# Two edits to a two-layer encoder trunk: four modulation dot products per plain tile of the first feed-forward part, and weight copies in program order on ACT in the last pair of the others

## The chip, the cores and the metric

The kernel runs on one core of one Trainium2 chip. It is one launch, and its time is what the device takes for it, in microseconds (us). A core has a matrix engine (PE, with its weight loads shown apart as PEld), a vector engine (DVE), a scalar engine (ACT), GpSimd (POOL) and a sync engine (SP), whose queue issues nearly all the transfers here. Each engine takes its own instructions in a fixed order, and semaphores hold an instruction until what it needs is there. Matmuls read their operands from SBUF and sum into PSUM.

## The reference

The input x is 512 rows of 1024 numbers. It passes through two layers; each is feed-forward, mixer, feed-forward. The mixer of layer 0 is a bidirectional Mamba-2 SSD, that of layer 1 is latent attention (MLA). The kernel counts these six sublayers as s = 0 (feed-forward), 1 (SSD), 2 and 3 (feed-forward), 4 (MLA), 5 (feed-forward). What matters here is the feed-forward and the modulation:

```python
D_MODEL, SEQ, DEPTH, D_FF = 1024, 512, 2, 2816

def modulate(x, g, shift, scale):
    return rms_norm(x, g) * (1.0 + scale[:, None, :]) + shift[:, None, :]

def swiglu(h, w_gate, w_up, w_down):
    return (jax.nn.silu(h @ w_gate) * (h @ w_up)) @ w_down

cond = jax.nn.silu(c)
for i in range(DEPTH):
    mod = (cond @ w_mod[i] + b_mod[i]).reshape(-1, 3, 3, D_MODEL)
    h = modulate(x, norm_g[i, 0], mod[:, 0, 0], mod[:, 0, 1])
    x = x + 0.5 * mod[:, 0, 2][:, None, :] * swiglu(h, ffn_w_gate[i, 0], ffn_w_up[i, 0], ffn_w_down[i, 0])
    h = modulate(x, norm_g[i, 1], mod[:, 1, 0], mod[:, 1, 1])
    x = x + mod[:, 1, 2][:, None, :] * mixer(h)
    h = modulate(x, norm_g[i, 2], mod[:, 2, 0], mod[:, 2, 1])
    x = x + 0.5 * mod[:, 2, 2][:, None, :] * swiglu(h, ffn_w_gate[i, 1], ffn_w_up[i, 1], ffn_w_down[i, 1])
```

Everything is float32. So `w_mod` is 2 x 1024 x 9216 numbers, 75 MB, and each of its 18,432 columns is used once, against one vector.

## The kernel before, in words

**Arithmetic.** A float32 product is made of three matmuls (`mm3`, L366 to L368): each operand is a high part plus a low part, and high x high, high x low and low x high are summed. The weights arrive as float32 (`raw`), ACT copies the high part (L169, a CAST to the matmul's type), and DVE subtracts it from `raw` to get the low part (L170).

**Weight units.** All weights are one long list of units of at most 128x1024 numbers (class `Units`). A unit is loaded by a transfer that SP issues (L113, at most three places `raw`, tag `raw`), then split by ACT and DVE into one of four places of a ring (`w`, RING = 4), and the matmuls read it there. So a split has to wait until the matmuls have let go of the unit four places earlier.

**A feed-forward sublayer** (`ffn`) goes through its 22 tiles of 128 hidden columns in four parts of 6, 6, 6 and 4 tiles (FF_PIECES; `pi` counts the parts). In a part, first the gate and up projections of its tiles, then their share of the down projection: eight output tiles into `dacc` for the first three parts, added to the residual X by DVE (L461), and `last()` (`lacc`) for the fourth, which also starts the next sublayer's norm. There are two ways for gate and up. A *plain* tile has two units (gate, up) and 24 matmuls of 512 columns for each, into `pgu`; then `gated` (silu on ACT, multiply L831 and low part L833 on DVE, high part L832 on ACT). A *pair* (`pair`, L784 to L815) does two tiles together in seven block products (`blk`) in place of eight, whose weights are sums of units: `cut_pair` makes them with ACT copies at L147 and DVE subtractions at L148. Its results `gs` go through silu (L802), a multiply (L803), the high part by ACT (L804) and the low part by DVE (L805) into `u`. The first sublayer (s = 0) uses plain tiles alone; s = 2, 3 and 5 use pairs from their fourth tile on. So "last pair" (`pi` = 3, `i` = 2) exists in s = 2, 3 and 5 alone. The four units of the down projection in `last()` go to places of their own (`wl`, tag `last`).

**Modulation.** The 144 dot products of `cond` with `w_mod` (8 blocks of 128 columns for each of 18 vectors) are DVE work: each is a transfer of 512 KB into `mraw` (L262, issued by SP, two places) and one multiply-and-sum over 128x1024 (L268), with a short read of the accumulator behind it. They are handed out in *ticks*: TICKS[s] = (dot products per plain tile, per pair, per output tile of the down projection). They stand in program order among themselves (`keep_in_program_order`), so that the transfers and the dot products keep their sequence. Each sublayer needs its own 24 before its norm and its gate; `finish_side` sees to that.

**Order of the work.** A scheduler orders each engine's instructions from the program, except where they are kept in program order, and in the first sublayer's start, which is written out by hand.

Of the kernel before, what the change touches and what calls it, by code (L numbers as in the profile page):

```python
# [22 lines left out]
FF_PIECES = (6, 6, 6, 4)  # L23
FF_MAX = max(FF_PIECES)
START = 3
TICKS = {0: (3, 1, 1), 2: (0, 0, 1), 3: (0, 0, 2), 5: (0, 0, 0)}
RIGHT = {0: (), 2: (), 3: (), 5: ()}
LATE = {4: 3, 2: 4}

# [47 lines left out]
class Units:  # L77
# [1 line left out]

    RAW_AHEAD, SPLIT_AHEAD = 3, 2  # L80

    def __init__(self, nc, raw_pool, w_pool):
        self.nc, self.raw_pool, self.w_pool = nc, raw_pool, w_pool
        self.todo, self.raw, self.split = [], {}, {}
        self.at = self.n_raw = self.n_split = 0
        self.held, self.in_ring = set(), {}
        self.places, self.over = {"raw": [], "raw4": []}, set()

    def add(self, src, n, kind="w"):
        self.todo.append((src, n, kind))  # L90
# [26 lines left out]
    def cut_pair(self, i, j, group, raw, t):  # L117
        nc = self.nc
        add, sub = nc.vector.tensor_add, nc.vector.tensor_sub
        minus = lambda out, x, y: nc.gpsimd.tensor_tensor(out, x, y, op=ALU.subtract)  # L120
        new = lambda: self.sum_pool.tile([P, 1024], F32, tag="sum", name="wsum", bufs=3)
        if raw is not None:
            group[j] = raw, i
        r = lambda j: group[j][0]
        if j < 2:
            x = raw
        elif j == 2:
            self.load(i + 2)
            group[3] = self.raw[i + 1], i + 1
            group["s1"], x = new(), new()  # L130
            group["s2"] = x
            add(group["s1"], r(2), r(3))
            (minus if "2" in POOL else sub)(x, group["s1"], r(0))
        elif j == 3:
            x = group["s1"]
        elif j == 4:
            x = new()
            (minus if "3" in POOL else sub)(x, r(0), r(2))
            self.over.update((group[0][1], group[2][1]))
        elif j == 5:  # L140
            x = new()
            (minus if "4" in POOL else sub)(x, r(1), group["s2"])
            self.over.add(group[1][1])
        else:
            x = r(3)
            self.over.add(group[3][1])
        nc.scalar.copy(out=t[:, 0], in_=x)  # L147
        (minus if "abcdefg"[j] in POOL else sub)(t[:, 1], x, t[:, 0].bitcast(F32))  # L148

    def cut(self, upto, early=False):  # L150
        while self.n_split < min(upto, len(self.todo)):
            i = self.n_split
            if self.todo[i][2] != "last":
                n = len(self.in_ring)
                if n - RING in self.held:
                    assert early, "a unit is wanted whose place is taken"
                    return
                self.in_ring[i] = n
            self.load(i + 1)
            _, n, kind = self.todo[i]  # L160
            raw = self.raw.pop(i)
            if kind != "last":
                t = self.w_pool.tile([P, 2, 1024], F32R, tag="w", name="w")
            else:
                t = self.last_pool.tile([P, 2, n], F32R, tag="last", name="wl")
            if isinstance(kind, tuple):
                self.cut_pair(i, *kind, raw, t)
            else:
                self.nc.scalar.copy(out=t[:, 0, :n], in_=raw[:, :n])  # L169
                self.nc.vector.tensor_sub(t[:, 1, :n], raw[:, :n], t[:, 0, :n].bitcast(F32))  # L170
                self.over.add(i)
            self.split[i] = t
            self.n_split += 1

    def next(self, ahead=True, hold=False):
        i = self.at
        self.at += 1
        self.load(i + 1)
        self.cut(i + 1)
        if hold:  # L180
            self.held.add(self.in_ring[i])
        if ahead:
            self.ahead()
        return self.split.pop(i)
# [19 lines left out]
class Trunk:  # L204
    def __init__(self, ctx, tc, d, subs):
        self.ctx, self.tc, self.nc, self.d = ctx, tc, tc.nc, d
        self.subs = subs
        pool = lambda name, **kw: ctx.enter_context(tc.tile_pool(name=name, **kw))
        self.const = pool("const", bufs=1)
        self.keep = pool("keep", bufs=1)  # L210
        self.raw_pool = pool("rawp", bufs=RAWS)
        self.w_pool = pool("wp", bufs=RING)
        self.units = Units(self.nc, self.raw_pool, self.w_pool)
        self.ps = pool("ps", bufs=3, space=PSUM)
        self.ps_c = pool("psc", bufs=3, space=PSUM)
        self.ps_s = pool("pss", bufs=2, space=PSUM)
        self.n_acc, self.wide = 0, False
# [424 lines left out]
    def ffn(self, s, nxt):  # L642
        nc, tc = self.nc, self.tc
        with ExitStack() as c:
# [28 lines left out]
            for pi, n in enumerate(FF_PIECES):  # L673
                for i in range(n):
                    if self.by_blocks(s, pi, i - i % 2):
                        if i % 2 == 0:
                            if self.factors == 0:
                                next(right)
                            self.pair(U[i:i + 2], wk, right)
                            self.ticks(TICKS[s][1])  # L680
                        continue
                    if first and pi == 0 and i < START:
                        self.gated(U[i], acc[2 * i], acc[2 * i + 1], full, wk)
                        self.ticks(TICKS[s][0])
                        continue
                    both = (i, i + 1) if pi == 0 and i == 0 else () if pi == 0 and i == 1 else (i,)
                    ws = [(self.units.next(), self.units.next()) for _ in both]
                    for ts in (halves if len(both) == 2 else (full,)):
                        nt = ts.stop - ts.start
                        for b, w in zip(both, ws):  # L690
                            pg, pu = (self.acc_tile("pgu") for _ in range(2))
                            self.norm_step(2 * b)
                            self.project(pg[:, :nt], w[0], ts)
                            if len(both) == 1:
                                self.ticks(TICKS[s][0] // 2)
                            self.norm_step(2 * b + 1)
                            self.project(pu[:, :nt], w[1], ts)
                            self.gated(U[b], pg, pu, ts, wk)
                    self.ticks(TICKS[s][0] - TICKS[s][0] // 2)
                    for _ in range(RIGHT[s].count((pi, i))):  # L700
                        next(right)
                while s not in self.gated_by:
                    self.tick()
                self.later = True
                if pi < len(FF_PIECES) - 1:

                    for ms in [(0, 1)] + [(m,) for m in range(2, KT)]:
                        part = []
                        for m in ms:
                            w = self.units.next()[:, :, :n * P].rearrange("p s (k c) -> p s k c", k=n)  # L710
                            part.append((w, self.acc_tile("dacc")))
                        for ks in (range(n - 1), (n - 1,)):
                            for w, ps in part:
                                for k in ks:
                                    self.mm3(ps, w, (k, slice(None)), U[k][0], U[k][1], k == 0, k == n - 1)
                        for m, (_, ps) in zip(ms, part):
                            self.residual(s, m, ps, full)
                            self.ticks(TICKS[s][2])
                else:
                    self.finish_side({0: 2, 2: 3, 3: 5, 5: 5}[s])  # L720
                    if nxt == 4:
                        v = self.rope.rearrange("p (n m) (c f) -> p n m c f", m=2, c=4)
                        self.tables = {"q": (v[:, 0, 0], v[:, 0, 1]), "k": (v[:, 1, 0], v[:, 1, 1])}
                        self.mla_tables()
                    self.last(s, nxt, n, lambda k: U[k])

    def right_tiles(self):
# [869 lines left out]
```

## Time and profile before

| | us |
|---|---|
| three timed runs: median (lowest to highest) | 2240.96 (2239.34 to 2241.18) |
| the profiled execution | 2238.92 |
| its span, first to last instruction | 2237.2 |
| PE busy in the span | 2192.6 (98%) |
| DVE busy | 1824.0 (82%) |
| ACT busy | 1109.3 (50%) |
| POOL busy | 239.7 (11%) |

The profiled execution is 1.7 us longer than its span, and 2.0 us below the median of the timed runs. Its mean granted TensorE clock was 0.991. The trace names a piece of work by its engine, its line and its tiles, as "PE dacc L368": a matmul of line 368 that writes `dacc`. SPq is SP's queue, where transfers are issued. "[4.20 <-ACT u L804]" behind an instruction says that its engine sat idle for 4.20 us and that ACT's write of `u` at line 804 ended it. The first sublayer's matmuls of `pgu` and `dacc` run from 65.6 us to 371.5 us of the span, in the parts `pgu` to 98.2, `dacc` to 132.1, `pgu` to 197.4, `dacc` to 230.0, `pgu` to 295.3, `dacc` to 328.0, `pgu` to 371.5.

### The profile page before, as it was taken

Reading aid. Unit: us, or ns where it says so; the run is one execution under the profiler, and the core shown is the slowest. Engines: PE = TensorE matmul, PEld = TensorE weight load, DVE = VectorE, ACT = ScalarE, POOL = GpSimd, SP = SyncE. Lnnn points to the kernel's source line nnn. Section 1 sums busy time; section 2 is a strip of 40 time slices with the busy share of each in tenths; the row PEclk is TensorE's granted clock in tenths of the full one; section 3 lists DMA queues with packets and bytes.
Section 4 is the critical chain, followed back from the end, with each engine's and each line's share of the span. In section 5 each row is a group of like instructions: output and inputs, shape, how many; then the busy total and the mean of one; then the engine's idle time right before and its main releaser. Section 6 shows DMA issues by size and latency. Waiting matters only on the chain.

```text
span 2237.2 us, 34479 instructions
## 1 busy us (share of the span) xinstructions
PE 2192.6 (98%) x13414; PEld 1932.0 (86%) x13414; DVE 1824.0 (82%) x2914; ACT 1109.3 (50%) x1890; POOL 239.7 (11%) x195
## 2 busy tenths in 40 slices
PE   8999999999999998999999999999999999999999
PEld 5888888878888877989999988899978888999989
DVE  7777667889888688889989879797779988877966
ACT  3322223687667675534435534353467875433433
POOL 0000000000000000010100001011046750011110
PEclk9999999999999999999999999999999999999999
DMA  8787776244434423253444144332220112333232
GB/s 297 224 276 249 234 248 222 85 128 142 132 122 134 141 95 120 90 168 114 169 161 160 58 141 137 109 100 90 78 68 14 39 39 76 97 102 104 93 105 76
DMA packets 87348, 292.93 MB, mean 131 GB/s; under 512 B 10192, under 2 KB 12880, under 8 KB 87184
## 3 DMA queue, kind: packets, MB, share of 16 engines
q1 hardware_dynamic: 86320, 288.79, 39.7%
q8 instruction: 105, 1.72, 0.3%
q10 hardware_dynamic: 864, 1.93, 0.2%
q14 instruction: 59, 0.48, 0.1%
HBM read 288.32 MB, written 2.36 MB: 130 GB/s over the span
## 4 chain that ended last, share of the span: by engine, by line
PE 83%; DVE 10%; DMA 3%; ACT 2%; issue 1%; POOL 1%; SPq 0%; ACTq 0%; DVEq 0%; POOLq 0%
PE blk L786 7%; PE blk L785 7%; PE blk L784 7%; PE dacc L368 5%; PE dacc L366 5%; PE dacc L367 5%; PE pgu L366 5%; PE pgu L367 5%; PE pgu L368 5%; PE inp L366 4%; PE inp L367 4%; PE inp L368 4%; DMA mraw<-in_wmod 2%; PE py L1075 2%; PE lacc L366 2%; PE oacc L366 2%
## 5 line engine op out<-in xcount | busy, mean ns | idle before, releaser
L169 ACT CAST w<-raw 128x1024 fp32r<-128x1024 f32 (+3 forms) x257 | 241.0, 945 | 343.9 <-PE dacc L368 110.4
L170 DVE TENSOR_TENSOR w<-raw,w 128x1024 fp32r<-128x1024 f32 (+3 forms) x257 | 280.0, 1095 | 49.9 <-ACT w L169 48.9
L786 PE MATMUL blk<-rf,w 128*128 128x256 f32 x864 | 245.7, 284 | 3.0 <-DVE w L148 3.0
L784 PE MATMUL blk<-rf,w 128*128 128x256 f32 x864 | 245.3, 284 | 0.8 <-ACT w L147 0.8
L785 PE MATMUL blk<-rf,w 128*128 128x256 f32 x864 | 245.2, 284 | 0.0
L268 DVE CUSTOM_DVE_ANT_0 mraw<-mraw,cond,small 128x1024 f32<-128x1024 f32 x144 | 182.4, 1280 | 54.1 <-DMA mraw<-in_wmod 53.8
L368 PE MATMUL dacc<-u,w 128*128 128x512 f32 x576 | 224.2, 389 | 0.6 <-DVE w L170 0.6
L367 PE MATMUL dacc<-u,w 128*128 128x512 f32 x576 | 224.3, 389 | 0.1
L366 PE MATMUL dacc<-u,w 128*128 128x512 f32 x576 | 224.2, 389 | 0.0
L366 PE MATMUL pgu<-Hhi,w 128*128 128x512 f32 (+1 forms) x592 | 208.4, 359 | 3.0 <-ACT Hhi L360 3.0
L368 PE MATMUL pgu<-Hhi,w 128*128 128x512 f32 (+1 forms) x592 | 210.2, 358 | 0.0
L367 PE MATMUL pgu<-Hlo,w 128*128 128x512 f32 (+1 forms) x592 | 209.8, 359 | 0.0
L786 PE MATMUL blk<-Hhi,w 128*128 128x256 f32 x648 | 183.4, 283 | 0.0
L785 PE MATMUL blk<-Hlo,w 128*128 128x256 f32 x648 | 183.4, 283 | 0.0
L784 PE MATMUL blk<-Hhi,w 128*128 128x256 f32 x648 | 183.3, 283 | 0.0
L786 PEld LDWEIGHTS blk<-rf,w 128*128 128x128 f32 x864 | 166.5, 193 | 3.8 <-DVE w L148 3.8
L120 POOL TENSOR_TENSOR wsum<-raw 128x1024 f32<-128x1024 f32 x27 | 83.0, 3076 | 795.1 <-DMA raw<-in_wpr 479.8
L784 PEld LDWEIGHTS blk<-rf,w 128*128 128x128 f32 x864 | 166.6, 193 | 1.0 <-ACT w L147 1.0
L785 PEld LDWEIGHTS blk<-rf,w 128*128 128x128 f32 x864 | 166.6, 193 | 0.0
L147 ACT CAST w<-wsum 128x1024 fp32r<-128x1024 f32 x108 | 111.9, 1044 | 94.0 <-PE dacc L368 39.8
L366 PE MATMUL inp<-Hhi,w 128*128 128x512 f32 x368 | 148.1, 402 | 0.0
L367 PE MATMUL inp<-Hlo,w 128*128 128x512 f32 x368 | 147.1, 400 | 0.0
(335 smaller groups left out, 5631.3 us busy)
## 6 DMA issues: line engine op xcount, KB each, us to landing
mraw<-in_wmod SPq DMA_DIRECT2D x144, 512.0 KB, 4.4
raw<-in_wpr SPq DMA_DIRECT2D x108, 512.0 KB, 3.5
raw<-in_wdn SPq DMA_DIRECT2D x96, 384.0 KB, 3.1
raw<-in_wgu SPq DMA_DIRECT2D x62, 512.0 KB, 4.1
raw<-in_wssd SPq DMA_DIRECT2D x48, 512.0 KB, 3.7
bc<-dpc SPq DMA_DIRECT2D x32, 512.0 KB, 4.0
raw<-in_wdn SPq DMA_DIRECT2D x16, 512.0 KB, 3.6
ee<-dex SPq DMA_DIRECT2D x32, 256.0 KB, 4.2
```

The source lines that it names most:

```text
L120: minus = lambda out, x, y: nc.gpsimd.tensor_tensor(out, x, y, op=ALU.subtract)
L147: nc.scalar.copy(out=t[:, 0], in_=x)
L169: self.nc.scalar.copy(out=t[:, 0, :n], in_=raw[:, :n])
L170: self.nc.vector.tensor_sub(t[:, 1, :n], raw[:, :n], t[:, 0, :n].bitcast(F32))
L268: return self.nc.vector.tensor_tensor_reduce(raw, raw, self.cond, 1.0, self.small[:, b:b + 1], ALU.mult, ALU.add, self.MC[:, s, j:j + 1])
L366: mm(ps, w[(slice(None), 0) + wsl], xhi, start=start, stop=False)
L367: mm(ps, w[(slice(None), 0) + wsl], xlo, start=False, stop=False)
L368: mm(ps, w[(slice(None), 1) + wsl], xhi, start=False, stop=stop)
L784: mm(o, wv[:, 0, e, k], hi[:, k], start=k == 0, stop=False)
L785: mm(o, wv[:, 0, e, k], lo[:, k], start=False, stop=False)
L786: mm(o, wv[:, 1, e, k], hi[:, k], start=False, stop=k == 3)
L1075: mm(py[64 * e:64 * e + 64, ch(c)], xd[:, dr, c, 64 * r:64 * r + 64], Es[e][:, dr, i], start=dr == 0, stop=dr == 1)
```

## The change

It has two edits.

**Ticks.** TICKS[0][0] goes from 3 to 4: in the first sublayer four dot products instead of three follow a plain tile, two of them before its up projection and two after. The list of 144 stays, so everything moves up: before the first pair (in s = 2) now 128 have been done, not 108. The 24 of s = 3 in the MLA layer's first feed-forward, of which 12 stood in s = 3 itself, are now all issued before it begins; s = 2 has 16 in place of 24. The 512 KB transfers move with them.

**Copies.** From the last pair of the fourth part on (s = 2, 3 and 5), until `last()` is called, the ACT copies of weights at L147 and L169 are kept in program order with respect to each other.

```diff
-TICKS = {0: (3, 1, 1), 2: (0, 0, 1), 3: (0, 0, 2), 5: (0, 0, 0)}
+TICKS = {0: (4, 1, 1), 2: (0, 0, 1), 3: (0, 0, 2), 5: (0, 0, 0)}
...
-    def __init__(self, nc, raw_pool, w_pool):
-        self.nc, self.raw_pool, self.w_pool = nc, raw_pool, w_pool
+    def __init__(self, tc, raw_pool, w_pool):
+        self.nc, self.raw_pool, self.w_pool = tc.nc, raw_pool, w_pool
+        self.pin = lambda i: i
...
-        nc.scalar.copy(out=t[:, 0], in_=x)
+        self.pin(nc.scalar.copy(out=t[:, 0], in_=x))
...
-                self.nc.scalar.copy(out=t[:, 0, :n], in_=raw[:, :n])
+                self.pin(self.nc.scalar.copy(out=t[:, 0, :n], in_=raw[:, :n]))
...
-        self.units = Units(self.nc, self.raw_pool, self.w_pool)
+        self.units = Units(tc, self.raw_pool, self.w_pool)
...
                     if self.by_blocks(s, pi, i - i % 2):
                         if i % 2 == 0:
+                            if pi == len(FF_PIECES) - 1 and i == n - 2:
+
+                                self.units.pin = tc.keep_in_program_order
                             if self.factors == 0:
                                 next(right)
                             self.pair(U[i:i + 2], wk, right)
...
                         self.mla_tables()
+                    self.units.pin = lambda i: i
                     self.last(s, nxt, n, lambda k: U[k])
```

The changed program has the same instructions. From line 82 on, its line numbers are one higher, and from `ffn` on five higher (L831 is L836, L804 is L809).

The first place is DVE in the second part of the first sublayer, from one plain tile's down-projection weights to the next (`g` is the tile's silu times up, `w` a unit's low part, `mraw` a dot product). Before:

```order
L268 ISA mraw,MC<-mraw,cond,small 128x1024
L268 ISA MC 128x1
L268 ISA mraw,MC<-mraw,cond,small 128x1024
L268 ISA MC 128x1
L170 TENSOR_TENSOR w<-raw,w 128x768
L268 ISA mraw,MC<-mraw,cond,small 128x1024
L268 ISA MC 128x1
L831 TENSOR_TENSOR g<-pgu,g 128x512
L170 TENSOR_TENSOR w<-raw,w 128x768
```

The same tile in the changed program:

```order
L269 ISA mraw,MC<-mraw,cond,small 128x1024
L269 ISA MC 128x1
L269 ISA mraw,MC<-mraw,cond,small 128x1024
L269 ISA MC 128x1
L171 TENSOR_TENSOR w<-raw,w 128x768
L269 ISA mraw,MC<-mraw,cond,small 128x1024
L269 ISA MC 128x1
L269 ISA mraw,MC<-mraw,cond,small 128x1024
L269 ISA MC 128x1
L290 SCALAR_TENSOR_TENSOR acol<-MC,small 128x8
L836 TENSOR_TENSOR g<-pgu,g 128x512
L171 TENSOR_TENSOR w<-raw,w 128x768
```

One more dot product stands between the low parts of the two units. Such tiles add up: ahead of the low part of the fifth down-projection unit in the third part stood 86 dot products of the 144, and now 104; ahead of the first gate unit of the second part it was 36, and is 37.

The second place is ACT at the end of s = 2, in the last pair and the start of `last()` (`gs` and `u` are the pair's results, `wl` the four weights of `last()`, `w` weights of the next sublayer). Before, from the condition vector's silu on:

```order
L257 ACTIVATE cond<-cond 128x1024
L802 ACTIVATE gs<-gs 128x256
L804 CAST u_7397<-gs 128x256
L802 ACTIVATE gs<-gs 128x256
L169 CAST w<-raw 128x1024
L804 CAST u_7396<-gs 128x256
L169 CAST wl<-raw 128x1024
L169 CAST w<-raw 128x1024
L802 ACTIVATE gs<-gs 128x256
L804 CAST u_7397<-gs 128x256
L169 CAST w<-raw 128x1024
```

And in the changed program:

```order
L807 ACTIVATE gs<-gs 128x256
L809 CAST u_7459<-gs 128x256
L170 CAST wl<-raw 128x1024
L807 ACTIVATE gs<-gs 128x256
L809 CAST u_7458<-gs 128x256
L170 CAST wl<-raw 128x1024 x2
L807 ACTIVATE gs<-gs 128x256
L170 CAST wl<-raw 128x1024
L809 CAST u_7459<-gs 128x256
L170 CAST w<-raw 128x1024
L305 ACTIVATE sqs<-X 128x256
```

The two copies for the next sublayer that stood ahead of the last results of the pair (u_7396 and u_7397, now u_7458 and u_7459) now stand behind them; the `wl` copies stand among them.

## Rows read from the trace of the kernel before

**Rows 1.** The page: busy time by engine, and the chain that ended last.
```profile
PE 2192.6 (98%) x13414; PEld 1932.0 (86%) x13414; DVE 1824.0 (82%) x2914; ACT 1109.3 (50%) x1890; POOL 239.7 (11%) x195
...
PE 83%; DVE 10%; DMA 3%; ACT 2%; issue 1%; POOL 1%; SPq 0%; ACTq 0%; DVEq 0%; POOLq 0%
```

**Rows 2.** Waits of PE, whole span: us in total, times, longest.
```profile
PE lacc L366 <- ACT u L804: 5.3, 2, 4.2
...
PE blk L786 <- DVE w L148: 3.0, 3, 1.5
```

**Rows 3.** Waits of PE in s = 3, where the third stands.
```profile
PE blk L784 <- ACT w L147: 0.8, 1, 0.8
```

**Rows 4.** Timeline of ACT, end of s = 2: start us, us, work, idle before.
```profile
1219.72 1.05 ACT L169 CAST w<-raw 128x1024 fp32r<-128x1024 f32 x1 [3.07 <-DMA raw<-in_wgu]
1220.67 0.40 ACT L804 CAST u<-gs 128x256 fp32r<-128x256 f32 x1
...
1225.60 0.41 ACT L804 CAST u<-gs 128x256 fp32r<-128x256 f32 x1 [1.98 <-DVE gs L803]
```

**Rows 5.** Timeline of PE, end of s = 2.
```profile
1226.05 1.23 PE L366 MATMUL lacc<-u,wl 128*128 128x256 f32 x4 [4.20 <-ACT u L804]
```

**Rows 6.** Timeline of DVE, first pairs of s = 3.
```profile
1374.68 1.28 DVE L268 CUSTOM_DVE_ANT_0 mraw<-mraw,cond,small 128x1024 f32<-128x1024 f32 x1
...
1376.22 1.28 DVE L268 CUSTOM_DVE_ANT_0 mraw<-mraw,cond,small 128x1024 f32<-128x1024 f32 x1
...
1377.42 1.22 DVE L148 TENSOR_TENSOR w<-wsum,w 128x1024 fp32r<-128x1024 f32 x1
```

**Rows 7.** Timeline of ACT, end of s = 5.
```profile
2210.62 1.05 ACT L169 CAST wl<-raw 128x1024 fp32r<-128x1024 f32 x1 [0.78 <-PE blk L786]
...
2213.29 0.41 ACT L804 CAST u<-gs 128x256 fp32r<-128x256 f32 x1 [1.31 <-DVE gs L803]
```

**Rows 8.** The page: the dot products, their transfers (KB, median us to landing).
```profile
L268 DVE CUSTOM_DVE_ANT_0 mraw<-mraw,cond,small 128x1024 f32<-128x1024 f32 x144 | 182.4, 1280 | 54.1 <-DMA mraw<-in_wmod 53.8
...
mraw<-in_wmod SPq DMA_DIRECT2D x144, 512.0 KB, 4.4
```

**Rows 9.** Tile `mraw`, 82 to 117 us: count, duration ns, first and last start.
```profile
L268 DVE CUSTOM_DVE_ANT_0 mraw<-mraw,cond,small x13: 1275/1283/1286, 82.2 to 116.8; 128x1024 f32<-128x1024 f32 x13
...
DMA to landing us min/median/max: 3.4/4.1/4.7
```

**Rows 10.** The same of 132 to 197.4 us.
```profile
L268 DVE CUSTOM_DVE_ANT_0 mraw<-mraw,cond,small x21: 1276/1283/1290, 132.2 to 194.4; 128x1024 f32<-128x1024 f32 x21
...
  DVE mraw L268: 11.1, 11
```

**Rows 11.** Timeline of SP's queue in the first `dacc` part.
```profile
107.57 7.97 SPq L262 DMA_DIRECT2D mraw<-in_wmod  x4
116.08 0.33 SPq L113 DMA_DIRECT2D raw<-in_wdn  x1
```

**Rows 12.** Timeline of PE there, and at the fifth `dacc` tile of the third part.
```profile
116.11 0.50 PE L368 MATMUL dacc<-u,w 128*128 128x512 f32 x1 [0.55 <-DVE w L170]
...
311.64 0.39 PE L366 MATMUL dacc<-u,w 128*128 128x512 f32 x1
```

**Rows 13.** Timeline of DVE: a dot product's start, then X and low parts.
```profile
129.22 1.29 DVE L268 CUSTOM_DVE_ANT_0 mraw<-mraw,cond,small 128x1024 f32<-128x1024 f32 x1 [2.22 <-DMA mraw<-in_wmod]
...
205.08 1.43 DVE L461 SCALAR_TENSOR_TENSOR X<-dacc,gcol,X 128x512 f32<-128x512 f32 x2 [2.64 <-PE dacc L368]
206.43 1.81 DVE L170 TENSOR_TENSOR w<-raw,w 128x768 fp32r<-128x768 f32 x2
```

**Rows 14.** Stretches: us, busy of each engine, clock, DMA share, GB/s.
```profile
132.00:197.40 65.40, 65.40 (x291) 54.13 (x289) 48.60 (x70) 17.70 (x23) 0.00 (x0) 1.00 0.84 269
132.00:328.00 196.00, 196.00 (x867) 162.28 (x866) 141.19 (x200) 50.73 (x64) 0.00 (x0) 1.00 0.78 250
```

**Rows 15.** The page: GB/s moved in each fortieth of the span (55.9 us).
```profile
GB/s 297 224 276 249 234 248 222 85 128 142 132 122 134 141 95 120 90 168 114 169 161 160 58 141 137 109 100 90 78 68 14 39 39 76 97 102 104 93 105 76
```

## The prediction

> **What bounds the kernel now.** I read the busy times first: PE works 98% of the span, DVE 82%, ACT 50%, and the chain that ended last lies on PE for 83% and on DVE for 10% [rows 1]. So an edit can only win back PE's few holes, or open new ones. Next I read what PE waits for. Two kinds bear on this change. PE's `lacc` waits 5.3 us for ACT's high parts of `u`, once for 4.2 and once for 1.1, and its `blk` waits 3.0 us for DVE's low parts of weights [rows 2], 0.8 us for ACT's copies [rows 3]. Last I read the first sublayer by tiles. Nothing in its parts holds PE for long; the hole that its weights leave is 0.55 us, for a low part, in the first `dacc` part [rows 12]. But there DVE is not idle by choice: it waits 53.8 us in the whole run for `mraw` to land [rows 8]. The first sublayer is where the extra dot products go, and it is also where the memory is busiest: 222 to 297 GB/s in the first seven fortieths, 14 to 169 in the rest [rows 15].
>
> **The copies.** At the end of s = 2 ACT comes to a copy for the next sublayer, whose raw unit has not landed; it idles 3.07 us until 1219.72, and only then makes the high part of `u` at 1220.67. Everything behind is late, the last high part is made at 1225.60 [rows 4], and PE stands 4.20 us until 1226.05 [rows 5]. In the changed order these copies stand behind the last `u`. What can be late next is the chain silu, multiply, high part, which follows the pair's last product. Where no foreign copy stood in the way, at the end of s = 5, ACT was released by that product at 2210.62 and made the last high part at 2213.29 to 2213.70, 3.1 us later [rows 7], and PE did not wait. The changed order is alike at all three ends: one `wl` copy between them. I therefore count the 5.3 us of `lacc` as gone and allow 1.0 us for what the new order leaves at the three ends together. The bounds: nothing, and three times the 1.1 us that the lesser of the two waits had, 3.3 us.
>
> **The dot products that leave s = 2 and s = 3.** The holes of `blk` in s = 3 lie beside the last two dot products: they start at 1374.68 and 1376.22 and hold DVE's low part of a weight until 1377.42 [rows 6]. With no dot product left in s = 3 I count 3.0 + 0.8 = 3.8 us as gone [rows 2, 3]; what comes after the last of them could stay, so 2 us is the low end. DVE's own work for 20 dot products, 20 x 1.28 = 25.6 us [rows 8], is merely moved: PE sets the pace where it leaves.
>
> Gain of both: 5.3 + 3.8 - 1.0 = 8.1 us.
>
> **The dot products that enter the first sublayer.** Here is the cost. A dot product needs a place of `mraw`, and there are two. The place's cycle is the transfer (median 4.1 us in the first `dacc` part, where the dot products were waited for) and the dot product of 1.28 us [rows 9], with about 0.1 us to issue: 5.5 us, or 2.76 us for each dot product of the two places. What I see is a little more: 13 of them from 82.2 to 116.8 us, so 34.6 / 12 = 2.88 us each [rows 9]. In the second part's gate and up tiles it was 62.2 / 20 = 3.11 us [rows 10], but there only 11 of the 21 were waited for, so this holds time in which DVE had to wait for PE. A plain tile takes PE 65.4 / 6 = 10.9 us [rows 14]. Three dot products of 2.88 us are 8.6 us and fit; four are 11.5 us and don't. DVE takes its instructions in order, so each tile pushes the weights' low parts back by 0.6 us and more; and the down projection, with one dot product for each of eight tiles in some 32.7 us, gives back some of it. What DVE has in hand is bounded by the ring of four units. The queue behind it is pushed too: SP's in-order issue stood 7.97 us over four `mraw` transfers, and the raw unit behind them was issued only at 116.08 [rows 11].
>
> The sum goes by one count, since the shortage lasts through two parts. Dot product 37 starts at 129.22 [rows 13], released by its transfer, and its place in the order is the same in the changed program. The fifth `dacc` unit of the third part stands behind dot product 104 there (86 before). At c us each, number 104 starts at 129.22 + 67 c, and behind it DVE does the dot product, two X of 1.43 us and one low part of 0.9 us [rows 13]: 3.6 us. PE wants this unit at 311.64 [rows 12]. It is late by 132.8 + 67 c - 311.6 us; at 2.67 us each it is just in time. I take c = 2.90, next to the waited-for stretch's 2.88: 132.8 + 194.3 - 311.6 = 15.5 us. That is lost in two pieces, in the `dacc` parts of the second and of the third part, each at the end of six tiles that fall short. After it come few dot products per unit, and nothing is given back to PE. The bounds: c = 3.11 gives 29.6 us; c = 2.76 gives 6.1 us; with the shortest landing of 3.4 us [rows 9] c is 2.4 us and the loss nothing.
>
> A second look at the same price, by bytes: from 132 to 328 us the core moved 250 GB/s, 49.0 MB [rows 14]; 18 more transfers of 0.524 MB make 58.4 MB. At the 297 GB/s of the busiest fortieth [rows 15] that is 197 us and just fits in the 196; at the 269 GB/s of the second part [rows 14] it is 217 us, 21 too long. So 15.5 lies inside what the traffic allows, and transfers that land faster than before aren't to be expected.
>
> **The sum.** Against the profiled execution of 2238.9 us: 2238.9 - 8.1 + 15.5 = 2246.3, say 2246 us. That execution is 2.0 us below the median of the timed runs, 2240.96, so the sum is 5 us or 0.2% above the median, and by the same count 7 us above its own kernel.
>
> **Rivals.** First, the cover holds. For it speaks that the ring lets DVE be four units ahead of PE, and a gate or up unit lasts PE 65.4 / 12 = 5.45 us [rows 14], more than any one wait for `mraw`; against it that it already fell behind once, at 116.11 [rows 12]. With c at or below 2.67 the first sublayer costs nothing and the time is 2238.9 - 8.1 = 2230.8 us; with 2.76 it is 2236.9. This decides at c = 2.75, where the loss is 5.7 us and the result leaves the noise on the fast side. A transfer that took no longer than it does alone would make this so: at the shortest landing of 3.4 us [rows 9] a place's cycle is 4.8 us and c 2.4. [...] The trace doesn't agree: the median here is 4.1 to 4.4 us [rows 8, 9], with the weights' transfers on the same engines.
>
> Second, it costs more. If the added traffic lengthens the landings, c is 3.11 and the loss 29.6 us: 2260.4 us. For it speaks the demand of 297 GB/s; against it that the dot products wait for each other and so spread the transfers.
>
> Third, the copies held in order open a hole of their own. A pinned copy of `wl` that waits for its raw unit stops ACT before the pair's last `u`, as the foreign copy did, at three ends. At 4.2 us each this is 12.6 in place of 1.0: 2258 us. It decides when a `wl` raw unit lands after the pair's last product; against it speaks that the last `wl` copy of s = 5 waited 0.78 us for a product and not for a transfer [rows 7].
>
> Fourth, the copies change nothing that PE feels, because PE waits for the late raw units one step on, in the next sublayer's first matmuls: the 5.3 us stay and the time is 2238.9 - 3.8 + 15.5 = 2250.6 us. For it speaks that a landing, and not ACT, ended the 3.07 us [rows 4]; against it that the next sublayer needs these units only after its norm.
>
> **How the numbers follow.** Forecast, c from 2.76 to 3.0: 0.5. Cover holds: 0.27. Dearer traffic: 0.13. The third and fourth: 0.1 together. A change under 0.2%, 4.5 us, can't be told from none here: the three timed runs lie 1.8 us apart. Faster needs a time below 2236.5, c below 2.75: 0.27. Slower needs one above 2245.4, c above 2.88: 0.28 of the forecast's 0.5, since its likeliest c lies just above this, 0.12 of the dearer traffic and 0.09 of the last two, 0.49. Between them 0.24. The range goes from the first rival's 2231 to the second's 2260; the forecast's own is 2237 to 2253.
>
> **What would show it.** In the changed profile: PE `dacc` waiting for DVE's `w` or for ACT's copy in the second and third parts, some 5 to 10 us in each, and the first `pgu` of the fourth part starting near 343 instead of 328 us; DVE's wait for `mraw` up from 53.8 us; no wait of `lacc` for `u` above 1 us; no `blk` wait at the start of s = 3. It would be wrong if the first sublayer's parts kept their lengths (then c was below 2.67), or if `lacc` still waited 4 us.

## The result, and the profile after

The changed kernel is slower: a median of 2255.27 us (2251.38 to 2258.43, 4 runs) against 2240.15 us (2237.76 to 2241.18, 4 runs) for the kernel before on the same chip, a ratio of 1.008 with a 95% interval of 1.0063 to 1.0097. The forecast was 2246 us in a range of 2231 to 2260, and slower at 0.49. The profiled execution, 2251.38 us, is the lowest of the four; it is 12.5 us above the profiled execution of before.

The page's busy time has moved little against [rows 1], since almost all work is the same; the chain has: PE's share of it fell from 83% to 72% and DMA's rose from 3% to 9%.

```profile
PE 2197.9 (98%) x13414; PEld 1932.6 (86%) x13414; DVE 1826.2 (81%) x2914; ACT 1106.7 (49%) x1889; POOL 240.0 (11%) x195
...
PE 72%; DVE 12%; DMA 9%; issue 3%; ACT 3%; POOL 1%; SPq 0%; DVEq 0%; ACTq 0%; POOLq 0%
```

Next come PE's waits over the whole span, the answer to [rows 2]: us in total, times, longest. The 5.3 us of `lacc` behind ACT's `u` are gone; a wait of 11.5 us, which was not there before, heads the list.

```profile
PE dacc L367 <- ACT u L837: 11.5, 3, 6.4
...
PE blk L791 <- DVE w L149: 2.4, 4, 0.8
...
PE lacc L368 <- DVE u L838: 1.4, 1, 1.4
```

How the 11.5 us come about is to be read from three engines at the end of the second part. DVE's timeline (start, duration, work, and in brackets the idle time before it with what ended it) shows four dot products, the last three of them, which are printed, waiting for their transfer, and the last tile's `g` only behind them:

```profile
200.24 1.29 DVE L269 CUSTOM_DVE_ANT_0 mraw<-mraw,cond,small 128x1024 f32<-128x1024 f32 x1 [1.02 <-DMA mraw<-in_wmod]
...
203.67 1.28 DVE L269 CUSTOM_DVE_ANT_0 mraw<-mraw,cond,small 128x1024 f32<-128x1024 f32 x1 [1.27 <-DMA mraw<-in_wmod]
...
206.20 1.28 DVE L269 CUSTOM_DVE_ANT_0 mraw<-mraw,cond,small 128x1024 f32<-128x1024 f32 x1 [1.24 <-DMA mraw<-in_wmod]
...
207.49 0.68 DVE L836 TENSOR_TENSOR g<-pgu,g 128x512 f32<-128x512 f32 x1
```

ACT makes the high part of `u` from it, after 9.04 us of waiting:

```profile
208.20 0.62 ACT L837 CAST u<-g 128x512 fp32r<-128x512 f32 x1 [9.04 <-DVE g L836]
```

And PE, which needs this `u` for the last matmuls of the first two output tiles of the down projection, stands 4.81 us. The third part has the same hole, 6.42 us long, and the fourth part's first `pgu` starts at 347.11:

```profile
208.87 0.79 PE L367 MATMUL dacc<-u,w 128*128 128x512 f32 x1 [4.81 <-ACT u L837]
...
212.42 0.63 PE L368 MATMUL dacc<-u,w 128*128 128x512 f32 x1
...
212.84 0.63 PE L369 MATMUL dacc<-u,w 128*128 128x512 f32 x1
...
215.57 0.39 PE L367 MATMUL dacc<-u,w 128*128 128x512 f32 x1
...
317.84 0.79 PE L367 MATMUL dacc<-u,w 128*128 128x512 f32 x1 [6.42 <-ACT u L837]
...
347.11 0.39 PE L367 MATMUL pgu<-Hhi,w 128*128 128x512 f32 x1
```

In the kernel before this was at 328.0, so the two parts cost 19.1 us. That is more than the holes: behind the first, after two wider steps, matmuls start 0.42 to 0.43 us apart until 215, in place of 0.23. From 208.87 to 215.57 there are 15 of them, at 0.227 us 3.4 us of work in 6.7. Behind the second hole it is the same, 15 from 317.84 to 324.65. The granted clock says so too, in the stretch of the first hole and behind the second (us, busy of each engine, clock, DMA share, GB/s); it was 1.00 there before:

```profile
198.00:215.00 17.00, 12.16 (x41) 9.13 (x40) 10.61 (x18) 3.44 (x5) 0.00 (x0) 0.81 0.80 258
317.00:350.00 33.00, 32.13 (x127) 25.98 (x128) 26.42 (x39) 8.19 (x9) 0.00 (x0) 0.89 0.80 266
```

The pace that the forecast rested on is one row of the tile `mraw`, from 132 to 345 us, beside what the dot products waited and the time to landing: 72 of them from 132.2 to 343.7, 211.5 / 71 = 2.98 us each, against the 2.88 of [rows 9] and the 2.90 assumed.

```profile
L269 DVE CUSTOM_DVE_ANT_0 mraw<-mraw,cond,small x72: 1270/1284/1287, 132.2 to 343.7; 128x1024 f32<-128x1024 f32 x72
...
  DVE mraw L269: 55.3, 47
...
DMA to landing us min/median/max: 3.4/4.3/6.7
```

Two of them carry the forecast's count: the 37th of the 144, which runs earlier than in the kernel before (129.22), and the 104th, which the count put at 323.5.

```profile
124.47 1.27 DVE L269 CUSTOM_DVE_ANT_0 mraw<-mraw,cond,small 128x1024 f32<-128x1024 f32 x1
...
324.60 1.29 DVE L269 CUSTOM_DVE_ANT_0 mraw<-mraw,cond,small 128x1024 f32<-128x1024 f32 x1 [3.32 <-DMA mraw<-in_wmod]
```

What the rest of the program makes of it is seen at two marks, PE's first `pgu` of s = 2 and of s = 5, in the kernel before and in the changed one:

```profile
887.94 1.22 PE L366 MATMUL pgu<-Hhi,w 128*128 128x256 f32 x4 [1.76 <-ACT Hhi L360]
...
1883.25 0.88 PE L366 MATMUL pgu<-Hhi,w 128*128 128x256 f32 x4 [1.29 <-ACT Hhi L360]
```

```profile
912.13 1.22 PE L367 MATMUL pgu<-Hhi,w 128*128 128x256 f32 x4 [1.76 <-ACT Hhi L361]
...
1894.10 0.83 PE L367 MATMUL pgu<-Hhi,w 128*128 128x256 f32 x4 [1.29 <-ACT Hhi L361]
```

So the first two sublayers lost 24.2 us: 19.1 to the fourth part; 3.6 in its `lacc`, most of it the 1.42 us hole and the matmuls behind it, 0.21 us apart until 399.5 in place of 0.12 ahead of it (the SSD sublayer's first matmul starts at 418.56 instead of 395.80); and 1.4 in the SSD sublayer. s = 2, 3 and 4 gave 13.3 back, and s = 5 lost 1.6: 12.5 us.

### The profile page after: what moved, and what is told of

Its sections match the earlier page's. It is cut to its first block, busy times and chain, and to the rows that moved or that the text cites. A ratio compares the mean times of both kernels' runs of the same rounds, so it can differ in the third digit from the quotient of the medians.

```text
span 2249.7 us, 34492 instructions
## 1 busy us (share of the span) xinstructions
PE 2197.9 (98%) x13414; PEld 1932.6 (86%) x13414; DVE 1826.2 (81%) x2914; ACT 1106.7 (49%) x1889; POOL 240.0 (11%) x195
## 4 chain that ended last, share of the span: by engine, by line
PE 72%; DVE 12%; DMA 9%; issue 3%; ACT 3%; POOL 1%; SPq 0%; DVEq 0%; ACTq 0%; POOLq 0%
DMA mraw<-in_wmod 9%; PE blk L791 6%; PE blk L790 6%; PE blk L789 6%; PE dacc L368 4%; PE dacc L367 4%; PE dacc L369 4%; PE inp L367 4%; PE inp L368 4%; PE inp L369 4%; PE pgu L367 2%; PE pgu L368 2%; PE pgu L369 2%; DVE mraw L269 2%; PE lacc L368 2%
## 5 line engine op out<-in xcount | busy, mean ns | idle before, releaser
L367 PE MATMUL dacc<-u,w 128*128 128x512 f32 x576 | 227.2, 394 | 11.8 <-ACT u L837 11.5
L368 PE MATMUL dacc<-u,w 128*128 128x512 f32 x576 | 227.1, 394 | 0.4 <-DVE u L838 0.3
L369 PE MATMUL dacc<-u,w 128*128 128x512 f32 x576 | 226.2, 393 | 0.4 <-DVE w L171 0.4
L149 DVE TENSOR_TENSOR w<-wsum,w 128x1024 fp32r<-128x1024 f32 x108 | 133.4, 1237 | 21.2 <-ACT w L148 21.2
```

Of the source, the lines that this page charges most:

```text
L367: mm(ps, w[(slice(None), 0) + wsl], xhi, start=start, stop=False)
L368: mm(ps, w[(slice(None), 0) + wsl], xlo, start=False, stop=False)
L369: mm(ps, w[(slice(None), 1) + wsl], xhi, start=False, stop=stop)
```

## The experiments

Each ran in turn with the kernel before on its own chip, whose median differed from chip to chip (2235.95 to 2240.15 us); so ratios are compared. A diff is against the changed kernel unless it says otherwise.

**The ticks alone** (against the kernel before).

```diff
-TICKS = {0: (3, 1, 1), 2: (0, 0, 1), 3: (0, 0, 2), 5: (0, 0, 0)}
+TICKS = {0: (4, 1, 1), 2: (0, 0, 1), 3: (0, 0, 2), 5: (0, 0, 0)}
```

Expected: 

> The kernel before with TICKS[0][0] = 4 alone, no pinned copies. In the changed kernel's trace the first sublayer lost 22.6 us to holes and slow matmuls (8.3 + 1.1 + 10.0 + 3.2), and the blk holes of s = 3 (6.4 us with the slow matmuls behind them) were gone. Theory A: the ticks make both of these, the pins make the ends of s = 2 and s = 3 good. Then this kernel loses 22.6, gains 6.4 and keeps the lacc holes: about 2240 + 16 = 2256 us, and lacc still waits about 4 us for ACT's u at the end of s = 2. Rival B: the late raw unit at the end of s = 2 was late because of the mraw transfers before it in SP's queue, so that the ticks alone remove it: about 2240 + 16 - 8 = 2248 us and no lacc wait above 1 us.

Measured: 2251.72 against 2235.95 us, ratio 1.0064 (1.005 to 1.0078), 16 us as theory A has it. PE's waits from 60 to 400 us, then from 900 to 1620:

```profile
PE dacc L366 <- ACT u L832: 13.0, 2, 6.8
```

```profile
PE lacc L366 <- ACT u L804: 3.1, 2, 2.0
```

Most of the slowdown is the ticks': their ratio is 1.0064, the changed kernel's 1.008. Neither theory had `lacc` quite right: it waits 2.0 us at the end of s = 2, where 4 or under 1 was expected. No `mraw` transfer stands in SP's queue there any more, and still ACT waits 2.32 us for a unit of the next sublayer ahead of the last results, where it was 3.07 [rows 4]. So those transfers were a part of the 4.2 us at most; the order on ACT makes a hole without them.

```profile
1240.34 1.05 ACT L169 CAST w<-raw 128x1024 fp32r<-128x1024 f32 x1 [2.32 <-DMA raw<-in_wgu]
```

**The pinned copies alone.**

```diff
-TICKS = {0: (4, 1, 1), 2: (0, 0, 1), 3: (0, 0, 2), 5: (0, 0, 0)}
+TICKS = {0: (3, 1, 1), 2: (0, 0, 1), 3: (0, 0, 2), 5: (0, 0, 0)}
```

Expected: 

> The changed kernel with TICKS[0][0] = 3 again, so the pinned copies alone. Theory A: the lacc holes go (6.95 us at the end of s = 2 with the slow matmuls behind, 1.3 us at the end of s = 3), and three holes of 1.1 us appear in the last pairs, where blk waits for DVE's low part; the blk holes of s = 3 stay: 2240 - 8.3 + 3.4 = 2235 us. Rival B (the ticks did it): the lacc holes stay and the three new ones come on top: 2243 us.

Measured: 2242.27 against 2235.95 us, ratio 1.0021 (1.0011 to 1.0031). The time is near rival B's, but its reason fell too: the `lacc` holes behind `u` are gone, as A said. Others came. PE's waits at the end of s = 2:

```profile
PE lacc L369 <- DVE wl L171: 2.6, 1, 2.6
PE blk L789 <- ACT w L148: 0.9, 1, 0.9
PE blk L791 <- DVE w L149: 0.8, 1, 0.8
```

Three engines show why `lacc` waits for a `wl` now. ACT has the high part of the second `wl` ready by 1221.63. But on DVE, ahead of its low part, stands the first step of the latent attention's position tables (`ang`, from a transfer `freq`), and that transfer lands only at 1223.1 us. DVE waits 2.81 us for it, and PE goes on when the low part is there:

```profile
1220.59 1.04 ACT L170 CAST wl<-raw 128x1024 fp32r<-128x1024 f32 x1
...
1223.13 0.37 DVE L1199 TENSOR_SCALAR ang<-freq,posf 128x16 f32<-128x16 f32 x2 [2.81 <-DMA freq<-in_freq]
...
1224.49 1.21 DVE L171 TENSOR_TENSOR wl<-raw,wl 128x1024 fp32r<-128x1024 f32 x1
...
1225.76 0.58 PE L369 MATMUL lacc<-u,wl 128*128 128x256 f32 x1 [2.65 <-DVE wl L171]
```

The transfer is issued by ACT at 1216.33 us here. In the changed kernel it is issued at 1111.1 and `ang` follows at 1114.6, so that this hole isn't there. The matmuls behind it start 0.21 us apart up to 1227.8, where those of `lacc` at this end start 0.12 us apart in the changed kernel; so up to there the hole costs an estimated 2.65 + 1.0 = 3.65 us of the 6.3 by which this kernel is slower. The pins open it only by moving that issue.

**Three places for `mraw` in the first sublayer**, both edits kept.

```diff
-            out = self.mod_pool.tile([P, KT * P], F32, tag="mraw", name="mraw", bufs=2)
+            out = self.mod_pool.tile([P, KT * P], F32, tag="mraw", name="mraw", bufs=3 if not self.later_ff else 2)
...
             self.mod_pool = pool("ffmod", bufs=1)
+            self.later_ff = s != self.subs[0]
```

Expected: 

> The changed kernel with three places for mraw in the first sublayer instead of two, nothing else. Theory A: two places set the pace (landing 4.4 + dot product 1.3 + issue 0.1 = 5.8 us for two, 2.9 us each); with three it is 1.9 us each, four fit in a tile of 10.9 us, the first sublayer loses under 4 us and the whole is about 2255 - 19 = 2236 us. Rival C: the memory is the bound (the parts want 298 GB/s, the busiest fortieth moves 297): the landings grow to about 6 to 7 us, the pace stays near 2.9 us, and the time stays above 2248 us.

Measured: 2236.6 against 2235.95 us, ratio 0.9996 (0.9986 to 1.0006): of the 0.8% nothing is left. Tile `mraw` from 132 to 345 us, and the stretch that the forecast's byte count was about:

```profile
L269 DVE CUSTOM_DVE_ANT_0 mraw<-mraw,cond,small x72: 1273/1279/1287, 133.7 to 344.4; 128x1024 f32<-128x1024 f32 x72
...
  DVE mraw L269: 10.4, 11
...
DMA to landing us min/median/max: 3.4/4.8/6.7
```

```profile
132.00:328.00 196.00, 196.00 (x866) 162.38 (x865) 153.36 (x221) 50.88 (x64) 0.00 (x0) 1.00 0.83 281
```

The waits of DVE fall from 55.3 to 10.4 us though the median landing takes 0.5 us longer, and PE has no idle moment in 196 us at 281 GB/s. Two places, not the memory, set the pace; rival C fell. One hole over 1 us is left in the first sublayer, in its first part, where dot products stand ahead of the low part of `u`:

```profile
PE dacc L368 <- DVE u L839: 2.2, 1, 2.2
```

**No transfers but the first of each sublayer.** The dot products read one block again and again, so the modulation isn't the reference's; their products go to a tile of their own, which nobody reads.

```diff
+        self.mraw_kept = None
+        self.mraw_out = self.mod_pool.tile([P, KT * P], F32, tag="mout", name="mout", bufs=1)
...
         if out is None:
-            out = self.mod_pool.tile([P, KT * P], F32, tag="mraw", name="mraw", bufs=2)
+            if self.mraw_kept is not None:
+                return self.mraw_kept
+            out = self.mraw_kept = self.mod_pool.tile([P, KT * P], F32, tag="mraw", name="mraw", bufs=1)
...
-        return self.nc.vector.tensor_tensor_reduce(raw, raw, self.cond, 1.0, self.small[:, b:b + 1], ALU.mult, ALU.add,
+        return self.nc.vector.tensor_tensor_reduce(self.mraw_out if raw is self.mraw_kept else raw, raw, self.cond, 1.0, self.small[:, b:b + 1], ALU.mult, ALU.add,
```

Expected: 

> The changed kernel with the mraw transfers left out after the first of each sublayer (the dot products read the same block again, so the modulation is not the reference's); the DVE work and its order are the same. Theory A and rival C both say that the transfers are the price: no wait of DVE for mraw is left, the first sublayer loses nothing and the time is about 2255 - 22.6 = 2232 us. Rival D: DVE's own work is (four dot products of 1.28 us in a row ahead of g, u and the low parts, in order): the holes of dacc stay near 5 us each and the time above 2245 us.

Measured: 2227.58 against 2235.95 us, ratio 0.9957 (0.9945 to 0.9969). Between 60 and 400 us the profile has no wait of PE at all. DVE's own work for four dot products a tile fits; rival D fell.

**Three places alone**, three ticks and no pins (the same edit on the kernel before).

Expected: 

> The kernel before (three ticks, no pinned copies) with three places for mraw in the first sublayer. Theory A: with three ticks two places were enough, PE had no hole there but one of 0.8 us, so this gains at most 1 us: 2236 us where before has 2236. The third place is worth something only with four ticks. Rival E: a third place helps by itself (the raw units behind mraw in SP's queue come earlier), 2230 us or less.

Measured: 2237.31 against 2237.88 us, ratio 1.0004 (0.9995 to 1.0013). As A said: a third place is worth nothing while three dot products fit.

**Three places, four ticks, no pins.**

```diff
-                                self.units.pin = tc.keep_in_program_order
+                                pass
```

on the kernel with three places. Expected: 

> Three places, four ticks, no pinned copies. In the kernel with pins the last pairs lost 1.0 + 3 x 1.1 = 4.4 us to blk holes and no lacc hole; with four ticks and no pins lacc lost 2.2 + 1.3 = 3.6 us and no blk hole at the ends. Theory A (the two edits add up): same as with pins within 1.5 us, about 2236 us. Rival F (the pins are a gain in themselves): 5 to 8 us slower than with pins, 2242 us.

Measured: 2233.38 against 2237.88 us, ratio 0.9984 (0.9975 to 0.9994). It is not slower than with the pins (0.9996, up to 1.0006), so F fell; whether it is faster the two intervals leave open.

**Three places, four ticks, plain copies pinned** (on the kernel with three places).

```diff
-        self.pin(nc.scalar.copy(out=t[:, 0], in_=x))
+        nc.scalar.copy(out=t[:, 0], in_=x)
```

Expected: 

> Three places, four ticks, and only the plain copies (L169) pinned, not the pair's (L147). Theory A: the pinned pair copies make the blk holes (ACT comes to them late, behind u), the pinned plain copies keep the foreign units behind the last u. So blk's three holes of 1.1 us go, lacc's don't come back: about 3 us faster than with all pins, 2233 us. Rival G: the blk holes come from the order of the u work itself, whatever is pinned: 2236 us, three holes as before.

Measured: 2232.95 against 2237.88 us, ratio 0.998 (0.9969 to 0.999). The `blk` holes at the three ends are gone and `lacc`'s have not come back. The interval overlaps that of all pins, so the times alone don't tell the two apart.

**Two places, three ticks, plain copies pinned**: the same line with TICKS[0][0] = 3. Expected: 

> Two places, three ticks, only the plain copies pinned. With all copies pinned this lost 3.6 + 4.2 + 0.7 + 1.1 + 1.1 = 10.7 us in new holes at the ends of s = 2, 3 and 5, and won the two lacc holes, 8.3 us. Theory A: the new blk holes go (6.5 us), the hole of lacc behind DVE's wl may stay (4.2 us); about 2236 - 4 = 2232 us. Rival G: nothing changes against all pinned, 2241 us.

Measured: 2232.14 against 2237.88 us, ratio 0.9979 (0.9968 to 0.9989), where all pins gave 1.0021. Of PE's waits in the whole span, `lacc` behind `u` is down to 0.6 us, and `blk` keeps what s = 3 had before [rows 2]:

```profile
PE blk L791 <- DVE w L149: 3.0, 3, 1.5
...
PE lacc L367 <- ACT u L809: 0.6, 1, 0.6
```

The new `blk` holes at the three ends are gone here as well, so the pair's copies were the wrong ones to pin. Not all of the 0.4% between this kernel and the one with all pins is theirs: the 2.65 us hole behind `freq` is gone too, whose transfer has landed by 1211.3 us here. The end of s = 5 in the changed kernel shows how they hurt. ACT makes a `u`, and only then the copies for the fifth and sixth of the pair's seven products, one after the other:

```profile
2211.67 0.41 ACT L809 CAST u<-gs 128x256 fp32r<-128x256 f32 x1 [0.49 <-DVE gs L808]
2211.98 1.99 ACT L148 CAST w<-wsum 128x1024 fp32r<-128x1024 f32 x2
```

and PE waits for the low part made from the first of them:

```profile
2214.34 0.39 PE L791 MATMUL blk<-rf,w 128*128 128x256 f32 x1 [0.76 <-DVE w L149]
```

**The best of it**: three places, three ticks in the first part and four in the other three of the first sublayer, plain copies pinned.

```diff
             for pi, n in enumerate(FF_PIECES):
+                tk = TICKS[s][0] - (first and pi == 0)
...
-                                self.ticks(TICKS[s][0] // 2)
+                                self.ticks(tk // 2)
...
-                    self.ticks(TICKS[s][0] - TICKS[s][0] // 2)
+                    self.ticks(tk - tk // 2)
```

Expected: 

> Three places for mraw in the first sublayer, three ticks in its first part and four in the other three, only plain copies pinned; all dot products are out of s = 3. With four ticks in every part this lost 4.7 us in the first dacc part, where the last u stood behind dot products. Theory: that hole goes, the others of the first sublayer stay small (1.7 us in the fourth part), s = 3 and the three ends have no hole over 1 us: about 2233 - 5 = 2228 us, a ratio to the kernel before of about 0.996. Rival: the lag only moves to the second dacc part, 2233 us.

Measured: 2228.89 against 2237.18 us, ratio 0.9958 (0.9946 to 0.997), faster than both kernels. PE's waits from 60 to 400 us:

```profile
PE lacc L368 <- DVE u L840: 0.7, 1, 0.7
PE lacc L367 <- ACT u L839: 0.6, 1, 0.6
```

**Out of s = 3 through s = 2**: two places, three ticks, plain pins, and

```diff
-TICKS = {0: (3, 1, 1), 2: (0, 0, 1), 3: (0, 0, 2), 5: (0, 0, 0)}
+TICKS = {0: (3, 1, 1), 2: (0, 0, 2), 3: (0, 0, 2), 5: (0, 0, 0)}
```

Expected: 

> Two places, three ticks, only plain copies pinned, and two dot products instead of one for each output tile of the down projection in s = 2, so that they are out of s = 3 without touching the first sublayer. Theory: the holes of s = 3 go (5.0 us), and what s = 2 loses depends on its down projection: a tile there lasts 4.1 us, two dot products in two places want 5.8 us, so that each part falls behind by some 8 x 1.7 = 14 us less the ring's cover, or the pairs behind catch up. I expect a loss of 5 to 10 us in s = 2: 2232 to 2238 us. Rival: the pairs, which have no dot products, give it all back, 2227 us.

Measured: 2249.46 against 2237.18 us, ratio 1.0053 (1.004 to 1.0065), far above the 2232 to 2238 us expected, and the rival's 2227 is out. PE's waits from 900 to 1240 us are of the pairs behind the down projection, whose copies and low parts stand behind the late dot products:

```profile
PE blk L789 <- ACT w L148: 6.8, 10, 2.2
PE blk L791 <- DVE w L149: 6.8, 9, 1.5
```

## Why the prediction was right, and where it was not

**The price of the dot products: right in place, near in size, wrong in the wait.** The pace of two places was forecast at 2.90 us and is 2.98. Number 104 starts at 324.60 us, where the count had 129.22 + 67 x 2.90 = 323.5; so by the count the fifth `dacc` unit of the third part is 16.6 us late and not 15.5, and the two parts lost 19.1. That the count came so near is in part luck. Number 37 doesn't keep its place in the order, as the step had it: it stands one place further forward, ahead of the second part's first gate unit, and starts 4.7 us earlier, which cancels most of the 5.8 us that the slower pace adds (324.60 - 124.47 = 200.1 us for the 67 steps, in place of 194.3). Two small slips of the working change nothing: a cycle of 5.5 us for two places is 2.75 us each and not 2.76, and at c = 2.75 the count gives a loss of 5.4 us and not 5.7.

The holes lie where they were put, in the `dacc` parts of the second and third part. But the step had PE waiting there for a unit's low part, five `dacc` tiles on. What came first was the last tile's `g`, which stands behind the same four dot products in DVE's order, and with it ACT's `u`, which the first `dacc` tiles need. I had counted the weights that are late and not the tile's own result. The wait for a low part is one of 0.4 us, in the first part, where it was 0.55. With two places, moving `g` ahead of the late dot products was not tried.

**A cost that I did not have.** Both holes cost more than their length, since the matmuls behind them start 0.43 us apart in place of 0.227: 3.3 us of the 8.1 at the first hole, 3.4 behind the second. The granted clock was 0.53 from 208.87 to 215.57 us and 0.51 from 317.84 to 324.65. So of the 19.1 us PE stood idle for some 12 and lost near 7 to the lower clock, for which the forecast had no term. It cuts the other way as well, in the kernel before: the stretches behind the 4.20 us hole of `lacc` and at the last holes of `blk` in s = 3 had a clock of 0.52 and 0.76. By estimate that is 6 x 0.48 = 2.9 and 7 x 0.24 = 1.7 us that went with the holes, and that the forecast's gain of 8.1 us didn't hold.

```profile
1226.00:1232.00 6.00, 5.95 (x28) 5.95 (x29) 3.76 (x13) 3.62 (x8) 0.00 (x0) 0.52 0.41 143
1396.00:1403.00 7.00, 5.39 (x30) 5.19 (x31) 6.75 (x10) 5.24 (x8) 0.00 (x0) 0.76 0.39 115
```

**The dot products out of s = 3: right.** The 3.0 and 0.8 us of `blk` are gone there; the kernel with three ticks and plain pins keeps them. They don't all lie beside the last two dot products, as the step said: two of the four holes end at 1396.85 and 1398.11 us, 20 us behind them, and went as well.

**The copies: this step failed.** It said that the 5.3 us of `lacc` go and that the new order leaves 1.0 us at the three ends together, and looked for it at `lacc` alone. The 5.3 us went. What was left out is that the edit also pins the pair's copies at L147, behind each `u` on ACT. In the changed kernel this makes three new holes of 0.8 us in `blk`, 2.4 us in place of the 1.0 allowed. One sign failed as well: `lacc` waits 1.42 us for a `u`, though in the first sublayer's fourth part, where DVE's low part of it stands behind a late dot product. The third rival, a pinned `wl` that waits for its raw unit, did not come: with the pins alone `lacc` has a hole of 2.65 us for a `wl`, but it is the transfer of `freq` that holds DVE there.

**The rivals.** The first, a cover that holds, fell with the pace: its 3.4 us landing is the shortest of a row whose median is 4.3 us. With a third place the cover does hold, but for 2.2 us. The second, dearer traffic, fell as well: with two places the landings kept their median, 4.3 us from 132 to 345 us in the kernel before and in the changed one. The fourth fell: no wait took the place of the 5.3 us in the next sublayer.

**The sum** came out 5 us low in the profiled execution (2246.3 against 2251.4). The first two sublayers lost 24.2 and not 15.5 us: 3.6 more in the two parts, 3.6 in the fourth part and 1.4 in the SSD sublayer, where the forecast had nothing, 8.7 together. s = 2, 3 and 4 gave back 13.3 and not 9.1, 4.2 more, though two of the new `blk` holes go off it; the clock behind the old holes is an estimated 4.6 of it, and about 1 us stays unexplained. s = 5 cost 1.6 where 1.0 had been allowed for all three ends. 8.7 - 4.2 + 1.6 - 1.0 = 5.1. So the total came near because misses of both signs met, the lost clock in the first sublayer and the clock given back in the later ones.

## What to carry to other kernels

Before more of a prefetched stream is put into a stage, compare the stage's time with the stream's own pace, (landing + use) / places, and not with the engine's busy share: here that pace is an estimated (4.3 + 1.28) / 2 = 2.8 us and was 2.98 measured, so 11.9 for four in a tile of 10.9. DVE was 74% busy in those tiles before [rows 14], a fourth dot product still found no room, and one more place gave it. When work on an in-order engine is late, list everything behind it, the stage's own results as well as its weights. Keep in program order only the instructions that stand in the wrong place: pinning the plain copies alone won 0.2%, pinning all lost 0.2%, in part because it also moved a small transfer into a place where DVE had to wait for it.

## What the runs showed of the hardware

The transfers got longer with a third place, from a median of 4.3 to 4.8 us, and the core still moved more in all: 281 GB/s from 132 to 328 us with PE busy throughout, against 250 in [rows 14] and 264 in the changed kernel with two places. I had not expected the clock to be lower behind one short hole and not behind another of its kind: behind the 1.42 us of `lacc` in the fourth part the clock of 5 us was 0.66, behind the 0.76 us of `blk` at the end of s = 5 it stayed at 1.00, and behind two holes of `blk` in s = 3 of the kernel before, 0.85 and 0.76 us and close together, it was 0.76. Nor is it the length alone: a single hole of 1.52 us, earlier in that same s = 3, ended at 1378.70 and left the clock at 1.00. What tells them apart wasn't tried.

```profile
1378.00:1385.00 7.00, 6.30 (x52) 6.30 (x53) 6.76 (x11) 3.81 (x6) 0.00 (x0) 1.00 0.23 75
...
395.00:400.00 5.00, 4.00 (x21) 4.00 (x22) 4.55 (x9) 0.81 (x3) 0.00 (x0) 0.66 0.90 308
2214.00:2218.00 4.00, 3.66 (x30) 3.67 (x31) 3.85 (x6) 0.92 (x1) 0.00 (x0) 1.00 0.02 4
```
